# Attention scores from 64-row products, the two maps in the two halves of the rows, in place of stacked 128-row operands

## The chip, the cores and the metric

The kernel runs on one core of one Trainium2 chip. The metric is device time in microseconds (us); less is better. Before the change three runs gave a median of 2869.48 us (2864.72 to 2870.2).

## What is computed

One inference step of a decoder trunk of two layers: a gated linear attention layer and a differential attention layer, each followed by an MLP with squared ReLU and by layer norms. 1024 prompt tokens with 16 meta tokens ahead of them, and 8 single tokens of running sequences, go through. The change lies in the differential attention of the prompt. There each of 8 heads has two maps, each with queries and keys of 64 dimensions:

```python
def diff_core(q, k, v, q_pos, k_pos, lam):
    s = jnp.einsum('bqhmd,bkhmd->bhmqk', q, k).astype(F32) * (DIFF_DH ** -0.5)
    mask = k_pos[None, :] <= q_pos[:, None]
    s = jnp.where(mask, s, -jnp.inf)
    p = jax.nn.softmax(s, axis=-1)
    a = p[:, :, 0] - lam * p[:, :, 1]
    return jnp.einsum('bhqk,bkhe->bqhe', a, v.astype(F32))
```

All data are f32.

## The kernel before, in words

Large products are made from rounded operands: a value is split into `hi`, its cast to the type fp32r, and `lo`, the rest (`split`, L182: a cast on ScalarE, a subtraction on VectorE), and a product of two such values is hi·hi + hi·lo + lo·hi (`mm3`, L186 to L189). Transposes and the products of attention weights with values stay in plain f32.

The stages run in this order: linear attention and its projections; output projection and MLP of the first layer, with the paged attention of the running sequences in the background; the input projection of the second layer (L1098 to L1145); the prompt's differential attention (L1238 to L1275); output projection (`w_out`, L883) and MLP of the second layer. A scheduler orders the instructions of each engine when the program is built, by the order of the code as priority and a time model; each engine then runs its own list in that order. Buffers come from pools, and a buffer is reused when its last reader is done.

Attention goes head by head, and within a head over eight tiles of 128 queries, in the order 7, 1, 5, 3, 6, 0, 4, 2 (L1243; 3, 2, 1, 0, 7, 6, 5, 4 in the last head). Tile t sees 16 + 128 (t + 1) keys.

`prep` (L1063) makes a head's operands. The raw keys and queries (`rqk`, `rkm`) lie with tokens on the partitions; TensorE transposes them into a PSUM bank `axt`, and `split` writes hi and lo with the 128 dimensions on the partitions: map 0 in rows 0 to 63, map 1 in rows 64 to 127. Then six moves for the queries and three for the keys (L1082 to L1084, L1093 to L1095, DMAs on POOL's queue from on-chip memory to itself) stack the operands by map: `k2[m]` holds the key's hi in 64 rows and its lo in the other 64, `q2[m]` the query's hi twice and `ql2[m]` its lo twice. Two products of 128 rows then give all four terms of one map (L1191, L1192). `prep` of the next head is issued at the first two tiles of a head (L1244 to L1249); that of head 0 between blocks of the input projection, whose last blocks are reordered for it (L1099, L1100, L1104). The operands of even and odd heads use different halves of `XH` and `XL`.

`tile_` (L1178) does one tile. Keys are cut into 1 to 3 chunks of at most 512 columns, 14 chunks a head. For each map and chunk: the two products into one PSUM bank `mmt`, and a VectorE reduction (L1195) that adds the mask, scales, writes the scores `as` to on-chip memory and keeps the row's extreme. ScalarE takes the exponentials of both maps (L1197), VectorE combines the maps (L1199 to L1201), TensorE transposes the result in groups of up to four blocks into `axt` (L1210), ScalarE copies these out (L1212), and TensorE multiplies them with the values into `smt` (L1215). After four tiles the results are copied out and their squares are summed (L1260 to L1262). POOL scales finished heads (L1227). In the last head the finished first half is transposed and split for the output projection (`o_fm`, L1229) while the second half runs.

PSUM has eight banks, shared out for the whole kernel: three `mmt` (L123), three `axt` (L124), two `smt` (L125).

Of the kernel before, what the change touches and what calls it, by code (L numbers as in the profile page):

```python
# [11 lines left out]
F32 = mybir.dt.float32  # L12
# [21 lines left out]
NEG = -1e30  # L34
# [77 lines left out]
def hybrid_step(ctx, tc, A, dbg=None, upto=9):  # L112
    nc = tc.nc
# [9 lines left out]
    mm = ctx.enter_context(tc.tile_pool(name="mm", bufs=3, space=PSUM))  # L123
    ax = ctx.enter_context(tc.tile_pool(name="ax", bufs=3, space=PSUM))  # L124
    sm = ctx.enter_context(tc.tile_pool(name="sm", bufs=2, space=PSUM))  # L125

    def mmt():
        return mm.tile([P, 512], F32, name="mmt")

    def axt():  # L130
        return ax.tile([P, 512], F32, name="axt")

    def smt():
        return sm.tile([P, 512], F32, name="smt")

    def cload(name, pool=cp):
        a, b = CCOL[name]
# [44 lines left out]
    def split(hi, lo, src, eng=V):  # L182
        S.copy(hi, src)
        return eng.tensor_tensor(lo, src, hi.bitcast(F32), op=ALU.subtract)  # L184
# [878 lines left out]
    def prep(h, raw, km):  # L1063

        kx, qx = raw[:, 0], raw[:, 1]
        xh, xl = (x.t[h % 2].rearrange("p a n -> p (a n)") for x in (XH, XL))
        w = NM + T
        k2 = [xh[:, :w], xh[:, w : 2 * w]]
        q2 = [xh[:, 2 * w : 2 * w + T], xh[:, 2 * w + T :]]
        kl_, ql2 = xl[:, :w], [xl[:, w : w + T], xl[:, w + T : w + 2 * T]]  # L1070
        kh_ = k2[0]
        move = nc.gpsimd.dma_start
        ps = axt()
        TE.transpose(ps[:, :NM], km, ident[:NM, :NM])
        split(kh_[:, :NM], kl_[:, :NM], ps[:, :NM])
        for c in range(2):
            ps = axt()
            for i in range(4):
                TE.transpose(ps[:, i * P : (i + 1) * P], kx[:, 4 * c + i, :], ident)
            cs = slice(NM + 512 * c, NM + 512 * c + 512)  # L1080
            split(kh_[:, cs], kl_[:, cs], ps)
        move(k2[1][64:], kh_[64:])  # L1082
        move(kh_[64:], kl_[:64])
        move(k2[1][:64], kl_[64:])  # L1084
        yield k2, q2, ql2
        for c in range(2):
            ps = axt()
            for i in range(4):
                TE.transpose(ps[:, i * P : (i + 1) * P], qx[:, 4 * c + i, :], ident)
            cs = slice(512 * c, 512 * c + 512)  # L1090
            split(q2[0][:, cs], ql2[0][:, cs], ps)
        for a, b in (q2, ql2):
            move(b[64:], a[64:])  # L1093
            move(b[:64], a[64:])
            move(a[64:], a[:64])  # L1095
        yield

    units, outs = {}, []  # L1098
    blocks = [(u, t) for u in range(10) for t in range(4)]  # L1099
    blocks += [(10, 0), (10, 1), (10, 2), (11, 0), (11, 1), (10, 3), (11, 2), (11, 3)]  # L1100
    for u, t2_ in blocks:
        if t2_ == 0:
            units[u] = [x.rearrange("p (k n) -> p k n", n=256) for x in kunit(wd, u * 256)]
        if (u, t2_) == (10, 3):  # L1104
            nxt = prep(0, *raws[0])
            with tc.issue_after(outs[-2 * NB]):
                head = next(nxt)
                next(nxt)
        hv, lv = units[u]
        ps = mmt()  # L1110
        for i in range(2):
# [66 lines left out]
    def tile_(h, t, out, vm, vx, k2, q2, ql2):  # L1178
        W = NM + P * (t + 1)
        nch = -(-W // 512)  # L1180
        step = -(-W // nch // 16) * 16
# [3 lines left out]
        mns, neg = st[:, 0, :], st[:, 1, :]  # L1185
        l = ls[:, t, h, :]
        ts_ = slice(t * P, (t + 1) * P)
        for m in range(2):
            for ci, (x, y) in enumerate(cuts):
                ps = mmt()[:, : y - x]  # L1190
                TE.matmul(ps, q2[m][:, ts_], k2[m][:, x:y], start=True, stop=False)  # L1191
                TE.matmul(ps, ql2[m][:, ts_], k2[m][:, x:y], start=False, stop=True)  # L1192
                w = y - x
                mk = cm[:, CW - w :] if y == W else cm[:, 0:1].broadcast_to([P, w])
                V.tensor_tensor_reduce(sc_[:, m, x:y], ps, mk, -0.125, -NEG if ci == 0 else mns[:, m : m + 1], ALU.add, ALU.min, mns[:, m : m + 1])  # L1195
# [39 lines left out]
        V.scalar_tensor_tensor(XL[:, h, cs], ps, gs, XH[:, h, cs].bitcast(F32), ALU.mult, ALU.subtract)  # L1235


    vnxt = load_v(0)  # L1238
    for h in range(8):
        if h:  # L1240
# [32 lines left out]
        o_fm(j, 1)  # L1273
    e.close()
    er.close()  # L1275

# [312 lines left out]
```

## Time and profile before

| | us |
|---|---|
| median of three runs | 2869.48 |
| the profiled execution, its own time | 2879.39 |
| its span, first to last instruction | 2877.6 |
| attention stage, first to last score reduction | 1793 to 2049 |
| busy in the span: TensorE, VectorE, ScalarE, POOL | 2752.2, 1964.2, 1084.7, 1161.8 |

Rows of the profile are read like this. In a group of lines: line, engine, operation, output<-inputs, shapes, count, then busy time and the mean of one in ns, then the idle time of the engine ahead of these instructions and what ended it. In a timeline: start and duration in us, engine, line, operation, tiles, shape, count; in square brackets the idle time before it and its releaser. In the table of stages: the stretch and its length, the busy time and number of instructions of TensorE, its weight loads, VectorE, ScalarE and POOL, then the granted TensorE clock, the DMA engines' busy share and GB/s. In the waits: who waited for whom, us in total, times, longest. PE is TensorE, PEld its weight loads, DVE VectorE, ACT ScalarE. The recorded duration of a matmul includes its way through the array; the pace of a stream is read from start to start.

### The profile page before, as it was taken

To read this page: it belongs to the slowest core of one execution; us is meant where nothing else is said; L and a number is where in the kernel's file an instruction comes from. 1 tells how busy PE (TensorE), PEld (TensorE's weight loads), DVE (VectorE), ACT (ScalarE), POOL (GpSimd) and SP (SyncE) were. 2 spreads that over 40 slices of the span, in tenths; PEclk is the share of its full clock that TensorE was granted. 3 is DMA by queue.
4 is the path that set the end of the run, shared out by engine and by line. 5 is a ranking of instruction groups with operands and counts; after the bars stand their busy time and mean duration, and the time that the engine had idled before them with its cause. 6 is when DMAs were issued, how large, how long until landed. Compare 5 with 4: busy or idle time off the path is not lost.

```text
span 2877.6 us, 51963 instructions
## 1 busy us (share of the span) xinstructions
PE 2752.2 (96%) x19625; PEld 2272.4 (79%) x19625; DVE 1964.2 (68%) x3048; ACT 1084.7 (38%) x2117; POOL 1161.8 (40%) x820
## 2 busy tenths in 40 slices
PE   8889999999999999999999999888999999999997
PEld 5666677997777777777798978878988889797985
DVE  2565544568887787777668721879638887878688
ACT  3233344242221221221341112767515546355553
POOL 1231212234344343433233321123236767777764
PEclk9899999999999999999999999999999999999998
DMA  7557751635798898888568995455334555554574
GB/s 242 181 177 269 253 169 46 238 96 158 283 344 304 311 354 305 329 321 298 213 217 317 360 343 140 107 114 132 119 103 88 110 129 116 132 122 111 130 189 88
DMA packets 277591, 579.66 MB, mean 201 GB/s; under 512 B 24710, under 2 KB 139980, under 8 KB 273244
## 3 DMA queue, kind: packets, MB, share of 16 engines
q1 hardware_dynamic: 252284, 520.66, 52.9%
q0 software_dynamic: 25056, 55.69, 11.1%
q8 instruction: 154, 2.52, 0.4%
q14 instruction: 97, 0.79, 0.1%
HBM read 531.16 MB, written 29.26 MB: 195 GB/s over the span
## 4 chain that ended last, share of the span: by engine, by line
PE 73%; DVE 9%; DMA 8%; issue 5%; POOL 2%; ACT 2%; SPq 0%; DVEq 0%; POOLq 0%; ACTq 0%
PE mmt L187 17%; PE mmt L188 17%; PE mmt L189 17%; PE smt L831 4%; PE axt L187 3%; PE axt L188 3%; PE axt L189 3%; DMA XL<-XL 2%; PE smt L1215 1%; DVE as L1195 1%; DVE pg L790 1%; DMA swt<-in_mlp_w 1%; PE smt L507 1%; DVE as L1201 1%; DMA rw<-in_mlp_w 1%
## 5 line engine op out<-in xcount | busy, mean ns | idle before, releaser
L175 POOL TENSOR_TENSOR wlo<-raw,whi 128x512 fp32r<-128x512 f32 x256 | 366.6, 1445 | 755.9 <-ACT whi L174 678.9
L188 PE MATMUL mmt<-wlo,XH 128*128 128x256 f32 (+1 forms) x1760 | 526.3, 300 | 4.4 <-POOL wlo L175 4.4
L187 PE MATMUL mmt<-whi,XH 128*128 128x256 f32 (+1 forms) x1760 | 525.0, 301 | 2.0 <-ACT Y L311 2.0
L187 PE MATMUL mmt<-XH,whi 128*128 128x512 f32 (+1 forms) x1216 | 436.8, 360 | 5.6 <-DVE HL L184 2.8
L189 PE MATMUL mmt<-whi,XL 128*128 128x256 f32 x1536 | 436.0, 285 | 0.0
L189 PE MATMUL mmt<-XH,wlo 128*128 128x512 f32 (+1 forms) x1216 | 432.9, 356 | 0.0
L174 ACT CAST whi<-raw 128x512 fp32r<-128x512 f32 x256 | 152.8, 619 | 596.4 <-PE mmt L189 185.4
L188 PEld LDWEIGHTS mmt<-wlo,XH 128*128 128x128 f32 x1760 | 333.7, 190 | 32.9 <-issue 17.7
L791 DVE TENSOR_REDUCE sc<-pg 128x16 f32<-128x1024 f32 x256 | 308.3, 1211 | 71.3 <-POOL pg L790 68.8
L187 PEld LDWEIGHTS mmt<-whi,XH 128*128 128x128 f32 x1760 | 332.1, 190 | 26.9 <-issue 12.2
L790 DVE TENSOR_TENSOR pg<-pg,qb 128x1024 f32<-128x1024 f32 x192 | 262.3, 1373 | 70.6 <-DMA pg<-in_cache_k 65.8
L188 PE MATMUL mmt<-XL,whi 128*128 128x512 f32 x768 | 306.2, 399 | 0.0
L189 PEld LDWEIGHTS mmt<-whi,XL 128*128 128x128 f32 x1536 | 291.2, 190 | 8.8 <-issue 8.0
L187 PEld LDWEIGHTS mmt<-XH,whi 128*128 128x128 f32 x1216 | 230.7, 190 | 52.8 <-issue 12.9
L790 POOL TENSOR_TENSOR pg<-pg,qb 128x1024 f32<-128x1024 f32 x64 | 164.3, 2569 | 258.7 <-DMA pg<-in_cache_k 179.9
L189 PEld LDWEIGHTS mmt<-XH,wlo 128*128 128x128 f32 x1216 | 230.7, 190 | 34.5 <-issue 2.1
L187 PE MATMUL mmt<-whi,HH 128*128 128x512 f32 x512 | 205.3, 402 | 4.5 <-DVE Y L1015 4.4
L189 PE MATMUL mmt<-whi,HL 128*128 128x512 f32 x512 | 204.5, 399 | 0.0
L188 PE MATMUL mmt<-wlo,HH 128*128 128x512 f32 x512 | 204.1, 399 | 0.0
L1436 POOL TENSOR_TENSOR wlo<-RW,whi 128x512 fp32r<-128x512 f32 x96 | 174.4, 1840 | 54.5 <-ACT whi L1435 54.5
L1436 POOL TENSOR_TENSOR wlo<-rw,whi 128x512 fp32r<-128x512 f32 x92 | 156.5, 1744 | 83.3 <-ACT whi L1435 68.1
L188 PEld LDWEIGHTS mmt<-XL,whi 128*128 128x128 f32 x768 | 145.0, 189 | 38.3 <-issue 7.1
(434 smaller groups left out, 5827.4 us busy)
## 6 DMA issues: line engine op xcount, KB each, us to landing
pg<-in_cache_k SPq DMA_DIRECT2D x256, 512.0 KB, 6.1
pg<-in_cache_v SPq DMA_DIRECT2D x256, 512.0 KB, 6.3
raw<-in_mlp_w SPq DMA_DIRECT2D x164, 256.0 KB, 4.6
swt<-in_mlp_w SPq DMA_DIRECT2D x32, 1024.0 KB, 5.2
rw<-in_mlp_w SPq DMA_DIRECT2D x116, 256.0 KB, 3.7
RW<-in_mlp_w POOLq DMA_DIRECT2D x96, 256.0 KB, 5.6
raw<-in_gla_w_in SPq DMA_DIRECT2D x48, 256.0 KB, 3.4
swt<-in_gla_w_in SPq DMA_DIRECT2D x12, 1024.0 KB, 5.1
```

Of the source, the lines that this page charges most:

```text
L174: S.copy(hi[:, c], raw)
L175: G.tensor_tensor(lo[:, c], raw, hi[:, c].bitcast(F32), op=ALU.subtract)
L187: TE.matmul(ps, ah, bh, start=first, stop=False)
L188: TE.matmul(ps, ah, bl, start=False, stop=False)
L189: return TE.matmul(ps, al, bh, start=False, stop=last)
L507: TE.matmul(ps[o : o + TS, :], lhs[:, k + i, :], t[:, i, c * 512 : (c + 1) * 512], start=k == 0, stop=k == nk - 2)
L790: eng.tensor_tensor(pg, pg, qb, op=ALU.mult)
L791: return V.tensor_reduce(sc[:, n, :], pg.rearrange("p (h d) -> p h d", d=64), op=ALU.add, axis=AX.X).ins
L831: m = TE.matmul(acc[i * TS : i * TS + 16, :256], w[r, n, :], pg[r, i * 256 : (i + 1) * 256], start=n == 0, stop=n == NPG).ins
L1195: V.tensor_tensor_reduce(sc_[:, m, x:y], ps, mk, -0.125, -NEG if ci == 0 else mns[:, m : m + 1], ALU.add, ALU.min, mns[:, m : m + 1])
L1201: V.scalar_tensor_tensor(sc_[:, 0, :W], sc_[:, 1, :W], neg[:, 0:1], sc_[:, 0, :W], ALU.mult, ALU.add)
L1436: G.tensor_tensor(lo[:, k, :], t, hi[:, k, :].bitcast(F32), op=ALU.subtract)
```

## The change

The stacked operands and the nine moves of each head go. `prep` only transposes and splits, into `ks` (hi and lo of the keys) and `qs` (hi and lo of the queries), one of four pieces at each of a head's tiles 2 to 5; that of head 0 stands whole before the last two blocks of the input projection, whose blocks run in plain order. In `tile_` each chunk has both maps at once: a pair of PSUM banks, and for each of the three terms hi·hi, hi·lo, lo·hi one product of 64 rows for map 0 (rows 0 to 63) and one for map 1 (rows 64 to 127), by turns. The fourth term, lo·lo, is no longer there. The two reductions follow the six products. For the attention stage the PSUM pools are closed and opened anew, as two pairs `prt` (four banks), two `axt` and two `smt`, and after it again as three, three and two.

```diff
+    def open_banks(**counts):
+
+        if banks:
+            banks["stack"].close()
+            banks.clear()
+        banks["stack"] = ctx.enter_context(ExitStack())
+        for name, n in counts.items():
+            banks[name] = banks["stack"].enter_context(tc.tile_pool(name=name, bufs=n, space=PSUM))
+
+    open_banks(mm=3, ax=3, sm=2)
+
+    def pairt():
+        return banks["pr"].tile([P, 2, 512], F32, name="prt")
...
-        k2 = [xh[:, :w], xh[:, w : 2 * w]]
-        q2 = [xh[:, 2 * w : 2 * w + T], xh[:, 2 * w + T :]]
-        kl_, ql2 = xl[:, :w], [xl[:, w : w + T], xl[:, w + T : w + 2 * T]]
...
-        move(k2[1][64:], kh_[64:])
-        move(kh_[64:], kl_[:64])
-        move(k2[1][:64], kl_[64:])
...
-        for a, b in (q2, ql2):
-            move(b[64:], a[64:])
-            move(b[:64], a[64:])
-            move(a[64:], a[:64])
...
+        ks, qs = [xh[:, :w], xl[:, :w]], [xh[:, w : w + T], xl[:, w : w + T]]
         ps = axt()
         TE.transpose(ps[:, :NM], km, ident[:NM, :NM])
+        split(ks[0][:, :NM], ks[1][:, :NM], ps[:, :NM])
+        for x, (hi, lo), at in ((kx, ks, NM), (qx, qs, 0)):
+            for c in range(2):
+                ps = axt()
+                for i in range(4):
+                    TE.transpose(ps[:, i * P : (i + 1) * P], x[:, 4 * c + i, :], ident)
+                cs = slice(at + 512 * c, at + 512 * c + 512)
+                split(hi[:, cs], lo[:, cs], ps)
+                yield ks, qs
...
-    blocks = [(u, t) for u in range(10) for t in range(4)]
-    blocks += [(10, 0), (10, 1), (10, 2), (11, 0), (11, 1), (10, 3), (11, 2), (11, 3)]
-    for u, t2_ in blocks:
+    for u, t2_ in ((u, t) for u in range(12) for t in range(4)):
...
-        if (u, t2_) == (10, 3):
-            nxt = prep(0, *raws[0])
+        if (u, t2_) == (11, 2):
             with tc.issue_after(outs[-2 * NB]):
-                head = next(nxt)
-                next(nxt)
+                head = list(prep(0, *raws[0]))[-1]
...
-        for m in range(2):
-            for ci, (x, y) in enumerate(cuts):
-                ps = mmt()[:, : y - x]
-                TE.matmul(ps, q2[m][:, ts_], k2[m][:, x:y], start=True, stop=False)
-                TE.matmul(ps, ql2[m][:, ts_], k2[m][:, x:y], start=False, stop=True)
...
+        for ci, (x, y) in enumerate(cuts):
+            w = y - x
+            mk = cm[:, CW - w :] if y == W else cm[:, 0:1].broadcast_to([P, w])
+            pair = pairt()
+            pss = [pair[:, m, :w] for m in range(2)]
+            for i, j in ((0, 0), (0, 1), (1, 0)):
+                for m in range(2):
+                    r = slice(64 * m, 64 * m + 64)
+                    TE.matmul(pss[m], qs[i][r, ts_], ks[j][r, x:y], start=i + j == 0, stop=i == 1)
+            for m in range(2):
+                V.tensor_tensor_reduce(sc_[:, m, x:y], pss[m], mk, -0.125, -NEG if ci == 0 else mns[:, m : m + 1], ALU.add, ALU.min, mns[:, m : m + 1])
...
+    open_banks(pr=2, ax=2, sm=2)
     vnxt = load_v(0)
...
                 if n == 0:
                     nxt = prep(h + 1, *raws[h + 1])
+                elif n < 5:
                     hnxt = next(nxt)
-                elif n == 1:
-                    next(nxt)
-                elif n == 3:
+                if n == 3:
                     vnxt = load_v(h + 1)
...
+    open_banks(mm=3, ax=3, sm=2)
```

More of the change, by code (lines that the diff above doesn't have):

```diff
@@ L122, in hybrid_step @@
     wrp = ctx.enter_context(tc.tile_pool(name="wrp", bufs=2))
-    mm = ctx.enter_context(tc.tile_pool(name="mm", bufs=3, space=PSUM))
-    ax = ctx.enter_context(tc.tile_pool(name="ax", bufs=3, space=PSUM))
-    sm = ctx.enter_context(tc.tile_pool(name="sm", bufs=2, space=PSUM))
+    banks = {}
+    def open_banks(**counts):
[8 more added lines that the diff above has]
+        return banks["pr"].tile([P, 2, 512], F32, name="prt")
     def mmt():
-        return mm.tile([P, 512], F32, name="mmt")
+        return banks["mm"].tile([P, 512], F32, name="mmt") if "mm" in banks else pairt()[:, 0]
     def axt():
-        return ax.tile([P, 512], F32, name="axt")
+        return banks["ax"].tile([P, 512], F32, name="axt")
     def smt():
-        return sm.tile([P, 512], F32, name="smt")
+        return banks["sm"].tile([P, 512], F32, name="smt")
     def cload(name, pool=cp):
@@ L1067, in prep @@
         w = NM + T
-        k2 = [xh[:, :w], xh[:, w : 2 * w]]
-        q2 = [xh[:, 2 * w : 2 * w + T], xh[:, 2 * w + T :]]
-        kl_, ql2 = xl[:, :w], [xl[:, w : w + T], xl[:, w + T : w + 2 * T]]
-        kh_ = k2[0]
-        move = nc.gpsimd.dma_start
+        ks, qs = [xh[:, :w], xl[:, :w]], [xh[:, w : w + T], xl[:, w : w + T]]
         ps = axt()
         TE.transpose(ps[:, :NM], km, ident[:NM, :NM])
[L1075 to L1081, printed above, removed]
@@ L1082, in prep @@
-        move(k2[1][64:], kh_[64:])
-        move(kh_[64:], kl_[:64])
-        move(k2[1][:64], kl_[64:])
[L1085 to L1091, printed above, removed]
-        for a, b in (q2, ql2):
-            move(b[64:], a[64:])
-            move(b[:64], a[64:])
-            move(a[64:], a[:64])
@@ L1096, in prep @@
-        yield
+        split(ks[0][:, :NM], ks[1][:, :NM], ps[:, :NM])
[7 more added lines that the diff above has]
+                yield ks, qs
     units, outs = {}, []
-    blocks = [(u, t) for u in range(10) for t in range(4)]
@@ L1176, in load_v, with tile_ @@
         return vm, vx
-    def tile_(h, t, out, vm, vx, k2, q2, ql2):
+    def tile_(h, t, out, vm, vx, ks, qs):
         W = NM + P * (t + 1)
```

3 lines of the change are left out of this document (removed).

## The prediction

> **What bounds the kernel now.** I read the page first, then the attention stage alone, because every line of the diff but one helper lies in it: the busy table by stage, the groups of lines within the stage, the waits, and the timelines of VectorE and TensorE around the first tile of each head.
>
> ```profile
> span 2877.6 us, 51963 instructions
> PE 73%; DVE 9%; DMA 8%; issue 5%; POOL 2%; ACT 2%; SPq 0%; DVEq 0%; POOLq 0%; ACTq 0%
> ```
> ```profile
> 1786.00:1820.00 34.00, 22.92 (x140) 19.95 (x141) 23.25 (x81) 17.59 (x42) 4.79 (x10) 0.87 0.59 136
> ...
> 1793.00:2045.00 252.00, 221.25 (x1546) 201.80 (x1544) 211.75 (x687) 179.47 (x427) 61.36 (x73) 0.94 0.49 112
> ```
>
> Over the whole span the chain is TensorE's. In the attention stage (about 1786 to 2067 us, the second row from the first score reduction to the end of the last head's scores) no engine is full: of 252 us TensorE is busy 221.25 and VectorE 211.75, in records whose TensorE ends are modelled. In the first stretch, with head 0's start, the granted clock is 0.87 against 0.94 over the stage: idle time costs some speed too. Both engines are near the limit, so what counts is which of the idle times end on something that the change removes.
>
> ```profile
> DVE as L1195 <- PE mmt L1192: 35.6, 30, 5.8
> ```
> ```profile
> L1195 DVE CUSTOM_DVE_ANT_0 as<-mmt,cmask 128x352 f32<-128x352 f32 x16 | 8.4, 522 | 22.2 <-PE mmt L1192 22.2
> ```
> ```profile
> 1793.29 0.52 DVE L1195 CUSTOM_DVE_ANT_0 as<-mmt,cmask 128x352 f32<-128x352 f32 x1 [5.79 <-PE mmt L1192]
> ...
> 1822.39 0.52 DVE L1195 CUSTOM_DVE_ANT_0 as<-mmt,cmask 128x352 f32<-128x352 f32 x1 [4.85 <-PE mmt L1192]
> ...
> 1853.76 0.53 DVE L1195 CUSTOM_DVE_ANT_0 as<-mmt,cmask 128x352 f32<-128x352 f32 x1 [2.95 <-PE mmt L1192]
> ...
> 1924.73 0.52 DVE L1195 CUSTOM_DVE_ANT_0 as<-mmt,cmask 128x352 f32<-128x352 f32 x1 [3.92 <-PE mmt L1192]
> ```
>
> VectorE waits 35.6 us for score products. 22.2 us of it stand before one form, the 352-column first chunk, which only tile 7 has, the tile with which heads 0 to 6 begin. The four long waits (17.5 us together) are the starts of heads 0, 1, 2 and 4. What TensorE waits for there:
>
> ```profile
> 1788.67 0.56 PE L1191 MATMUL mmt<-XH 128*128 128x352 f32 x2 [2.68 <-DMA XH<-XH]
> 1792.48 0.96 PE L1192 MATMUL mmt<-XH,XL 128*128 128x352 f32 x2 [3.25 <-DMA XL<-XL]
> ...
> 1819.01 0.63 PE L1191 MATMUL mmt<-XH 128*128 128x352 f32 x1 [3.71 <-issue]
> ...
> 1922.19 0.59 PE L1191 MATMUL mmt<-XH 128*128 128x352 f32 x2 [3.58 <-DMA XH<-XH]
> ```
>
> These are the moves that stack the operands (L1082 to L1084, L1093 to L1095): chains of copies from on-chip memory to itself, issued from POOL. Head 0's chain ends at 1792.48, though the projection before it was done some 8 us earlier:
>
> ```profile
> 1784.41 0.28 PE L188 MATMUL mmt<-wlo,XH 128*128 128x256 f32 x1
> 1784.53 0.28 PE L189 MATMUL mmt<-whi,XL 128*128 128x256 f32 x1
> ```
>
> The 1819.01 wait is put down to "issue", but the move line names its waiters:
>
> ```profile
> L1095 POOL DMA_DIRECT2D XL<-XL x8: 509/512/523, 1785.7 to 2014.3; - x8
> ...
>   PE mmt L1191: 6.3, 2
>   PEld mmt L1192: 6.0, 4
>   PE mmt L1192: 5.0, 4
>   PEld mmt L1191: 3.8, 1
> ```
>
> That is 21.1 us of TensorE waiting for the moves, seen from the other side.
>
> **The moves (removed).** Nine copies a head go, 72 in all, with POOL's 0.51 us for each issue (37 us of POOL, whose 61.36 busy us are not on the path). The transposes, casts and subtractions stay: five pieces a head before and after (16 keys, then four of 512 columns). Their last one is now all that a head's start needs, and they are spread over tiles 2 to 5 of the head before, so it is ready about three tiles early. For head 0 the whole of prep stands before two projection blocks, 2 x 48 matmuls at 0.12 us (start to start in the fence above), 11.5 us, which cover these. I take back 20 of the 22.2 us: a little stays, since a head's first reduction still needs its own products. What is late next is VectorE itself, with 211.75 us of work that the change doesn't touch.
>
> **The products.** Per head and map the keys sum to 8 x 16 + 128 x 36 = 4736 columns. Now: two products of 128 rows, two maps, 18944 columns a head. The steady pace:
>
> ```profile
> 1838.75 0.46 PE L1191 MATMUL mmt<-XH 128*128 128x464 f32 x1
> 1839.05 0.37 PE L1192 MATMUL mmt<-XH,XL 128*128 128x464 f32 x1
> 1839.26 0.37 PE L1191 MATMUL mmt<-XH 128*128 128x448 f32 x1
> 1839.47 0.36 PE L1192 MATMUL mmt<-XH,XL 128*128 128x448 f32 x1
> ```
>
> Start to start 0.21 us for 464 columns, 0.457 ns a column, so 8.66 us a head and 69 us in the stage. Afterwards there are three products of 64 rows per map. If the two halves of the rows run side by side, that is three times instead of four: 52 us, 17 less. If they run one after the other it is six: 104 us, 35 more. No 64-row matmul and none of this rounded type with fewer than 128 rows is in the trace. The nearest rows are two 16-row products in different row groups, in plain f32:
>
> ```profile
> L619 PE MATMUL axt<-gT,wg x16: 587/640/692, 93.7 to 388.1; 16*128 16x512 f32 x16
> ```
> ```profile
> 93.68 0.70 PE L619 MATMUL axt<-gT,wg 16*128 16x512 f32 x2
> ```
>
> Two matmuls, each recorded with at least 0.587 us, lie together within 0.70 us: they run side by side. I take the side-by-side value, with some doubt about the type, and keep both ends. It matters less than it looks: in the forecast VectorE sets the pace, and 17 us fewer on TensorE only shorten the other waits for products (35.6 - 22.2 = 13.4 us at most).
>
> The Trainium skill speaks against this step in TensorEngine Tiling (Array Packing), Key Properties: a change of tiling mode drains TensorE. The row that bears on it is the return from the 16-row products:
>
> ```profile
> 388.58 0.50 PE L187 MATMUL mmt<-XH,whi 128*128 128x512 f32 x1
> 388.92 0.40 PE L188 MATMUL mmt<-XL,whi 128*128 128x512 f32 x1
> 389.15 0.40 PE L189 MATMUL mmt<-XH,wlo 128*128 128x512 f32 x1
> ```
>
> The first slot is 0.34 us, the next 0.23: 0.11 us for the change. Today's scores already pay 0.09 when they follow f32 work (0.30 against 0.21 at 1838.75). If leaving the mode costs another 0.11, that is 112 chunks x 0.11 = 12 us more of TensorE, hidden while VectorE is the bound. By the rule taken alone the sum would be the same with 12 us less reserve; the rule and the row agree that there is a price.
>
> **Banks.** Scores go from three single banks to two pairs, transposes from three to two. A pair holds two reductions, about 1.2 us of VectorE's work, and TensorE refills it in 3 x 0.457 x 338 = 0.46 us plus the signals: no wait of its own. The transposes:
>
> ```profile
> L1212 ACT COPY aT<-axt 128x512 f32<-128x512 f32 (+2 forms) x112 | 51.9, 491 | 41.7 <-PE axt L1210 41.4
> ...
> L184 DVE TENSOR_TENSOR XL<-axt,XH 128x512 fp32r<-128x512 f32 (+1 forms) x34 | 20.1, 593 | 3.1 <-ACT XH L183 3.1
> ```
>
> 112 copies and 34 splits take turns in these banks. With one bank fewer, a transposition can wait for one copy more. Bounds: 0 and 112 x 0.49 = 55 us of TensorE waiting; the lower end is nearer, because copies today wait 41.4 us for transposes and hardly the other way:
>
> ```profile
> PE axt L1210 <- ACT aT L1212: 0.3, 1, 0.3
> ```
>
>  I charge 4 us to the end. Below nothing it can't go.
>
> Between the stages the pools are closed and opened again. That this is no barrier is shown by the pool that replaces the stage's buffers:
>
> ```profile
> L1315 SPq DMA_DIRECT2D rw<-in_diff_w_out x16: 327/364/722, 2001.8 to 2121.6; - x16
> ```
> ```profile
> 2043.13 0.41 PE L1191 MATMUL mmt<-XH 128*128 128x320 f32 x1
> ...
> 2045.79 0.35 PE L187 MATMUL mmt<-whi,XH 128*128 128x256 f32 x1
> ```
>
> Its first load goes out at 2001.8, while the stage that stands before it in the code still computes. And today's output projection starts only after the last scores, so its banks come free at the same point. Nothing is charged; if this were a barrier, the projection would lose its place under the last tiles (2045.8 to 2066), up to 20 us.
>
> **The sum.** -20 (head starts) + 4 (transposes) = -16 us, against the profiled execution's 2879.39 us, 9.9 above the median of the runs shown (2869.48). Carried over to that median: **2853.5 us**. The forecast's own range adds the 13.4 us of other waits below (2840) and 10 us more for banks, mode changes and the order of the instructions, which a scheduler sets anew when the program is built, above (2863.5).
>
> **Rivals.** *The halves run one after the other* (slower). The row for it: none; against it the pair at 93.68. TensorE then has 221 + 35 = 256 us, above VectorE, and becomes the bound. Of its 31 idle us in the stage, some 17 go with the moves and 14 stay: 270 us for 252, less the 6 that head 0's start still gives, +12 us: 2881.5. It decides as soon as a pair of 64-row matmuls takes over about 1.6 times one of them (3 x 1.6 = 4.8 against 4, TensorE then at 235 + 14 us of 252, where hardly anything is left of the gain in the running heads). Chance 0.16.
>
> *Each weight load waits for the matmul in its own half.* A load of 128 columns fits beside a matmul within (1.05 - 0.28) / 7 = 0.11 us today:
>
> ```profile
> 1868.16 1.05 PE L1215 MATMUL smt<-whi,aT 128*128 128x128 f32 x8
> ```
>
>  Unhidden it costs 3 x 0.11 a chunk: 3 x (0.155 + 0.11) = 0.80 us against 0.62 now, 20 us more of TensorE; 241 + 14 is 255 for 252, and with the start's 6 about 2866.5. Against it:
>
> ```profile
> 1000.27 0.50 PE L189 MATMUL mmt<-whi,HL 128*128 128x512 f32 x1
> ```
> ```profile
> 1000.38 0.19 PEld L187 LDWEIGHTS mmt<-whi,HH 128*128 128x128 f32 x1
> ```
>
> The next load runs 0.11 us into a matmul on the same rows. The Trainium skill states the rule in TensorE: Matmul & The Clock Gate, The mechanism: loads overlap running matmuls only where the row group differs. This trace disagrees. Chance 0.06.
>
> *The banks take the gain.* If two transposition banks and pairs held to the end cost 20 us instead of 4, little is left: 2869.5. For it: TensorE issues in order, and everything behind a waiting transposition waits too. Against: the 0.3 us that transposes wait for copies today. Chance 0.10.
>
> *A pool barrier* at the end: 2853.5 + 16 = 2869.5. Chance 0.04.
>
> **Chances.** The forecast holds 0.64. A measurement of this kernel can tell about 0.2% (5.7 us) from no change. Faster by more: nearly all of the forecast and the lucky parts of the rivals, 0.68. Within it: the forecast's high end and the middle of the last three rivals, 0.15. Slower: most of the serial rival and the unlucky parts of the others, 0.17. The range reaches to 2838 below and, with half of the serial rival, to 2882 above.
>
> **What would show it.** Right: no move and no long wait at head starts; the first score reduction within about 2 us of the last projection matmul (1793.3 now); 64-row matmuls of two maps starting a few ns apart, three such pairs in about 0.47 us; VectorE over 90% busy from there to the last scores, which end some 16 us earlier. Wrong: score matmuls start one full matmul apart; VectorE waits for products in the middle of heads; transposes wait for copies; the projection starts after the last transposition. One cause of long waits stays in any case:
>
> ```profile
> 1881.48 1.09 PE L1210 MATMUL axt<-c_ident,as 128*128 128x128 f32 x4 [4.56 <-DVE as L1201]
> ```
>
> It ends on a VectorE pass (L1201) that the change doesn't touch.

## The result, and the profile after

The changed kernel takes 2876.7 us (median of 22 runs) where the kernel before takes 2869.46 (22 runs): 1.0023 times the time, 95% interval 1.0014 to 1.0032. It is slower, by some 7 us; 16 us faster was forecast. The profiled executions differ by 5.5 us in span. First line of the page of after, then two rows of its table of stages: the start, and first score reduction to last scores.

```profile
span 2883.1 us, 52158 instructions
```
```profile
1786.00:1820.00 34.00, 24.48 (x166) 19.93 (x167) 24.20 (x84) 17.79 (x45) 0.00 (x0) 0.78 0.09 24
1791.00:2042.00 251.00, 224.55 (x1757) 182.55 (x1757) 210.47 (x688) 177.60 (x425) 29.04 (x12) 0.95 0.16 46
```

POOL's busy time has halved (29.04 for 61.36) and DMA's share fell from 0.49 to 0.16: the moves are gone. Yet the stage is as long as it was, TensorE is no less busy, and VectorE idles 40.5 of 251 us where it idled 40.3 of 252. One idle time was swapped for another. The groups of VectorE lines in the attention stage of after (busy and mean | idle ahead and its releaser):

```profile
L1195 DVE SCALAR_TENSOR_TENSOR as<-as,ast 128x1040 f32<-128x1040 f32 (+7 forms) x62 | 61.8, 996 | 0.8
L1189 DVE CUSTOM_DVE_ANT_0 as<-prt,cmask 128x272 f32<-128x272 f32 (+5 forms) x128 | 58.6, 495 | 17.5 <-DMA out_v_rows_p<-qo 13.0 <-PE prt L1187 4.5
L1189 DVE CUSTOM_DVE_ANT_0 as<-prt,cmask,ast 128x352 f32<-128x352 f32 (+5 forms) x96 | 52.2, 576 | 10.0 <-PE prt L1187 10.0
L196 DVE TENSOR_TENSOR XL<-axt,XH 128x512 fp32r<-128x512 f32 (+1 forms) x35 | 20.4, 582 | 9.3 <-ACT XH L195 9.3
...
L1256 DVE TENSOR_REDUCE oss<-smt 128x4 f32<-128x512 f32 x15 | 10.4, 693 | 4.8 <-ACT smt L1255 4.8
L1193 DVE RECIPROCAL ast<-ls 128x1 f32<-128x1 f32 x62 | 9.8, 158 | 9.6 <-ACT as L1191 9.3
```

Before, 22.2 us stood ahead of the 352-column first chunk alone, at the starts of heads. Now there are short waits all over: for scores, for the casts of the preparation (L195), for exponentials, for squares, each kind 0.6 to 2 us a head. By heads, VectorE idles 5.0 to 5.5 us in each of heads 1 to 6.

The start kept most of its delay. TensorE has the first scores at once, VectorE does not take them:

```profile
1786.06 0.43 PE L1187 MATMUL prt<-XH 64*128 64x352 f32 x2 [0.72 <-ACT qo L1108]
1786.33 0.32 PE L1187 MATMUL prt<-XL,XH 64*128 64x352 f32 x2
1786.49 0.32 PE L1187 MATMUL prt<-XH,XL 64*128 64x352 f32 x2
```
```profile
1791.31 0.53 DVE L1189 CUSTOM_DVE_ANT_0 as<-prt,cmask 128x352 f32<-128x352 f32 x1 [13.04 <-DMA out_v_rows_p<-qo]
```

The row puts the wait down to the landing of the projection's last output, so some buffer that the reduction needs lies where that output was. Which one is not shown: e8_start, below, moves the score buffers and keeps the wait. From the end of the projection's last output copy it is 5.3 us to this reduction (1786.0 to 1791.3), where it was 7.8 before (1785.5 to 1793.3): behind the wait for the moves stood another. The granted clock of the start fell from 0.87 to 0.78.

The first rows also answer the question of the halves: each row is two matmuls (x2), and the next pair follows 0.16 us later, 0.457 ns by 352. They run side by side, a pair in 0.16 us at this pace; only the first pair holds its slot for 0.27.

Where the difference lies, from the timelines (first and last score reduction; last addition of the output projection; end):

| us | before | after | difference |
|---|---|---|---|
| to the first score reduction | 1793.3 | 1791.3 | -2.0 |
| first to last score reduction | 255.8 | 253.1 | -2.7 |
| from there to the end of the output projection | 127.0 | 136.4 | +9.4 |
| rest | 701.5 | 702.3 | +0.8 |

The forecast put some 6 us of its gain into the first line, the rest into the second, and nothing into the third (a pool barrier there was one of its rivals).

### The profile page after: what moved, and what is told of

Same layout as the page of the kernel before. It is cut to its first block, busy times and chain, and to the rows that moved or that the text cites. A ratio compares the mean times of both kernels' runs of the same rounds, so it can differ in the third digit from the quotient of the medians.

```text
span 2883.1 us, 52158 instructions
## 1 busy us (share of the span) xinstructions
PE 2755.9 (96%) x19849; PEld 2253.8 (78%) x19849; DVE 1987.5 (69%) x3048; ACT 1082.8 (38%) x2117; POOL 1112.3 (39%) x748
## 4 chain that ended last, share of the span: by engine, by line
PE 69%; DVE 14%; DMA 7%; issue 5%; ACT 2%; POOL 2%; SPq 1%; DVEq 0%; POOLq 0%; ACTq 0%
PE mmt L199 17%; PE mmt L200 16%; PE mmt L201 16%; PE smt L843 4%; PE axt L199 2%; PE axt L200 2%; PE axt L201 2%; DVE as L1189 2%; DVE as L1195 1%; DVE pg L802 1%; DMA rw<-in_mlp_w 1%; PE smt L1209 1%; DVE XH L196 1%; ACT as L1191 1%; DVE RX L1406 1%
## 5 line engine op out<-in xcount | busy, mean ns | idle before, releaser
L1431 POOL TENSOR_TENSOR wlo<-RW,whi 128x512 fp32r<-128x512 f32 x96 | 167.7, 1794 | 58.6 <-ACT whi L1430 58.5
```

Source lines behind the costliest of these rows:

```text
L1431: G.tensor_tensor(lo[:, k, :], t, hi[:, k, :].bitcast(F32), op=ALU.subtract)
```

## The experiments

Times are medians with the ratio to the kernel before on the same chip, whose medians there lay between 2869.4 and 2873.1 us; so small differences are read from the ratios; "stage" is first to last score reduction of the profiled execution, "tail" from there to the end of the output projection, "held" what the 64 combinations of two maps take beyond the median of their own length (explained below).

| kernel | us | ratio, 95% interval | stage | held | tail |
|---|---|---|---|---|---|
| before | 2869.5 | 1 | 255.8 | 11.7 | 127.0 |
| after | 2876.7 | 1.0023 (1.0014 to 1.0032) | 253.1 | 10.5 | 136.4 |
| e1_no_moves | 2835.1 | 0.9880 (0.9855 to 0.9905) | 217.4 | 2.7 | 127.5 |
| e2_old_banks | 2881.9 | 1.0035 (1.0019 to 1.0050) | 265.2 | 2.9 | 130.7 |
| e3_singles | 2878.3 | 1.0026 (1.0011 to 1.0040) | 256.5 | 8.0 | 136.4 |
| e4_prep_early | 2874.3 | 1.0006 (0.9992 to 1.0021) | 250.7 | 8.3 | 136.1 |
| e5_form_alone | 2870.4 | 0.9998 (0.9982 to 1.0014) | 254.0 | 0.7 | 130.0 |
| e6_full_rows | 2873.4 | 1.0005 (0.9989 to 1.0021) | 248.0 | 10.6 | 136.9 |
| e8_start | 2869.6 | 0.9995 (0.9980 to 1.0010) | 249.9 | 10.5 | 135.8 |
| e9_doubled | 2870.9 | 0.9994 (0.9979 to 1.0010) | 252.4 | 4.9 | 126.2 |
| e10_pair | 2860.3 | 0.9969 (0.9954 to 0.9984) | 236.6 | 8.6 | 137.3 |
| e11_spread | 2831.5 | 0.9866 (0.9846 to 0.9886) | 218.0 | 0.0 | 126.1 |
| e12_norm_split | 2862.9 | 0.9988 (0.9974 to 1.0001) | 241.4 | 0.0 | 135.2 |
| e13_sum | 2852.4 | 0.9951 (0.9930 to 0.9971) | 243.1 | 0.3 | 128.7 |
| e14_two_banks | 2848.5 | 0.9923 (0.9904 to 0.9942) | 224.3 | 7.7 | 138.8 |
| e15_order | 2834.0 | 0.9878 (0.9857 to 0.9898) | 218.9 | 5.9 | 130.5 |
| e16_three_banks | 2842.8 | 0.9900 (0.9883 to 0.9918) | 238.6 | 0.7 | 126.6 |
| e17_before_split | 2870.0 | 1.0001 (0.9985 to 1.0017) | 253.8 | 8.1 | 127.5 |
| e18_full_early | 2861.2 | 0.9972 (0.9958 to 0.9985) | 236.4 | 8.6 | 136.7 |
| e19_three_early | 2840.0 | 0.9903 (0.9885 to 0.9920) | 231.5 | 1.4 | 127.9 |

**First round: the moves, and the banks undone.** e1_no_moves is the kernel before with

```diff
-        k2 = [xh[:, :w], xh[:, w : 2 * w]]
-        q2 = [xh[:, 2 * w : 2 * w + T], xh[:, 2 * w + T :]]
+        k2 = [xh[:, :w]] * 2
+        q2 = [xh[:, 2 * w : 2 * w + T]] * 2
...
-        move(k2[1][64:], kh_[64:])
...
-            move(a[64:], a[:64])
```

so both maps are computed from the same unstacked operands. It leaves out each map's own scores; so do e6_full_rows, e10_pair, e11_spread, e14_two_banks, e15_order and e18_full_early.

> The kernel before with the nine moves of each head left out and nothing else: both maps then use the same pair of operands, so the scores are those of a sum of both maps and the output is not the reference's; the instructions of all engines but the moves stay. Theory A (the moves' waits were worth what their rows said, and the changed kernel gives it back in its banks): 12 to 20 us below before. Rival B (the waits for moves stood where another wait stands anyway): between 5 below and 2 above.

It saved 34 us, beyond every expectation. Stage row and two groups:

```profile
1790.40:2007.80 217.40, 208.21 (x1575) 194.83 (x1576) 202.65 (x698) 178.64 (x431) 28.76 (x13) 0.99 0.20 58
```
```profile
L1188 DVE CUSTOM_DVE_ANT_0 as<-mmt,cmask 128x272 f32<-128x272 f32 (+5 forms) x128 | 61.6, 494 | 7.3 <-PE mmt L1185 4.4 <-DMA out_v_rows_p<-qo 2.6
```

VectorE is busy 93%, TensorE 96%, the clock is 0.99. Of 38 us less in the stage 25 are VectorE's idle time (40.0 to 14.8) and 9 its held combinations. So the moves were worth more than the waits at the head starts, and the rest of the change must cost some 40 us.

e2_old_banks and e3_singles are the changed kernel with single banks, three for scores and three for transpositions throughout, or four and two (the second part of this edit is e3_singles'):

```diff
-            pair = pairt()
-            pss = [pair[:, m, :w] for m in range(2)]
+            pss = [mmt()[:, :w] for m in range(2)]
...
-    open_banks(pr=2, ax=2, sm=2)
+    open_banks(mm=4, ax=2, sm=2)
```

> The changed kernel with the old banks for the whole kernel: three single score banks, three for transposes, two for results, no pools opened anew; each map's products go to a bank of their own. Theory A (two transposition banks and pairs take the gain): 10 to 18 us below before. Rival B (the place of prep, the halves or a wait that was hidden take it): not more than 3 us below before, about as the changed kernel.

> The changed kernel with four single score banks in place of two pairs, transposes still in two banks. If the release of both banks of a pair at once costs the time: 6 or more us faster than the changed kernel, so at or below before. If the transposition banks do, or neither: as the changed kernel, 5 to 9 us above before.

Both stayed slow, and I took the banks to be cleared. That was too quick: with single banks the second map often has none free and products run alone (355 of 663 in the trace of e2_old_banks, none of 672 in after), so undoing the banks uncovers another cost. In e2_old_banks TensorE is busy 258.75 of 265.2 us.

e4_prep_early prepares in the first two tiles (`if n < 2: next(nxt); hnxt = next(nxt)`).

> The changed kernel with prep of the next head at the first two tiles of a head, where it was before, two pieces at each. If the spread over four tiles puts VectorE's subtractions where it waits for them: 4 or more us faster than the changed kernel. If the two transposition banks are the limit, four pieces close together press harder on them: the same or 2 to 6 us slower.

2874.3 against 2876.7: the intervals overlap.

**Second round: the form of the products.** e5_form_alone is e1_no_moves with the three products of 64 rows, maps by turns, in single banks. e6_full_rows is the changed kernel with products of 128 rows, both maps from the same operands:

```diff
-            for i, j in ((0, 0), (0, 1), (1, 0)):
-                for m in range(2):
-                    r = slice(64 * m, 64 * m + 64)
-                    TE.matmul(pss[m], qs[i][r, ts_], ks[j][r, x:y], start=i + j == 0, stop=i == 1)
+            for m in range(2):
+                for i in range(2):
+                    TE.matmul(pss[m], qs[i][:, ts_], ks[0][:, x:y], start=i == 0, stop=i == 1)
```

> The kernel before with its moves left out (as in e1_no_moves), its old banks, old preparation in two tiles and old block order, but with the three products of 64 rows, the maps by turns, in place of two of 128 rows on operands of one map; both maps correct. It differs from e1_no_moves (2835 us) only in the form of the score products. Theory A (every visit of TensorE to the 64-row form costs some 0.18 us at its two edges, 82 to 112 visits, 15 to 20 us, and VectorE is starved by it): 2860 to 2882. Theory B (the form is cheap; what eats the gain is where the preparation, the blocks and the banks were put): 2833 to 2848.

> The changed kernel with everything as it is (pair banks, preparation over five tiles, plain block order, no moves), but each map's score as two products of 128 rows on the same pair of operands, so both maps get the same scores, which are not the reference's. It differs from the changed kernel (2877) only in the form of the score products. Theory A (the 64-row form): 2832 to 2850, the other edits being worth about 5 us together. Theory B (placement and banks): 2865 to 2880.

Both came out slow, so both theories failed as the only cause: the form alone loses the 34 us, and everything but the form loses them too. Row of e5_form_alone, and some of its score products:

```profile
1786.70:2040.70 254.00, 250.21 (x1778) 205.84 (x1779) 207.55 (x701) 181.21 (x432) 30.73 (x13) 0.96 0.18 50
```
```profile
1859.87 0.45 PE L1188 MATMUL mmt<-XH 64*128 64x384 f32 x1
1860.16 0.33 PE L1188 MATMUL mmt<-XL,XH 64*128 64x384 f32 x1
1860.33 0.34 PE L1188 MATMUL mmt<-XH,XL 64*128 64x384 f32 x1
```

TensorE is full, 250.21 of 254, 42 us more than in e1_no_moves. Part of it is halves that run alone (x1, above), for want of a bank; the pair banks of the changed kernel cure that. The other part is the visit to this form (a visit is a stretch of score products between others). In after, one between output products:

```profile
1901.42 0.83 PE L1209 MATMUL smt<-whi,aT 128*128 128x128 f32 x6
1902.18 0.47 PE L1187 MATMUL prt<-XH 64*128 64x448 f32 x2
1902.49 0.36 PE L1187 MATMUL prt<-XL,XH 64*128 64x448 f32 x2
1902.69 0.37 PE L1187 MATMUL prt<-XH,XL 64*128 64x448 f32 x2
1902.98 0.49 PE L1209 MATMUL smt<-whi,aT 128*128 128x128 f32 x2
```

Six output products at 0.11 us end at 1902.08; the first score starts 0.10 later. Its slot is 0.31 and the last 0.29, where 448 columns stream in 0.20. The first output product behind holds its slot for 0.21 in place of 0.11 (0.49 for two, of which the last is recorded with 0.28). That is 0.1 each on entering, on the first pair, on leaving and on the first product behind (0.06 where that is a transposition), nearly 0.4 us a visit. In e1_no_moves the same edges cancel:

```profile
1850.98 0.60 PE L1079 MATMUL axt<-c_ident,rqk 128*128 128x128 f32 x4
1851.33 0.38 PE L1184 MATMUL mmt<-XH 128*128 128x272 f32 x1
1851.55 0.29 PE L1185 MATMUL mmt<-XH,XL 128*128 128x272 f32 x1
1851.67 0.28 PE L1184 MATMUL mmt<-XH 128*128 128x256 f32 x1
1851.79 0.28 PE L1185 MATMUL mmt<-XH,XL 128*128 128x256 f32 x1
1851.91 1.04 PE L1203 MATMUL axt<-c_ident,as 128*128 128x128 f32 x8
```

The score starts 0.08 before the transpositions' pace would allow (1850.98 + 4 x 0.109), loses 0.09 in its first slot, leaves at its own pace, and so does the transposition behind. In after TensorE visits the scores 79 times between 1795 and 2030 us: 79 x 0.4 = some 30 us, more than the 17 that side by side saves. That the Trainium skill (TensorEngine Tiling (Array Packing), Key Properties) has a mode change drain TensorE agrees with these rows; it gives no price.

e8_start opens the pool of score buffers ahead of its neighbours:

> The changed kernel with the pool of the score buffers opened ahead of its neighbours, so that the first score buffer need not lie on the projection's last output buffer, whose landing the first reduction waited 5.2 us for. If that wait is a cost of its own: 4 to 5 us less than the changed kernel, 2871 to 2874. Rival: another buffer of the new pool then waits for the same landing (the mask or the small tiles), or the projection's tail sets the start anyway: 2875 to 2879.

2869.6 us, 7 less than after, but not for the reason given: its first reduction still waits for the same landing (1780.02, 5.1 us after its scores). Most of the gain lies in the projection, as waits in after (first row) and the groups of TensorE in after and in e8_start show:

```profile
POOL vm L1158 <- SPq L769: 9.4, 1, 9.4
```
```profile
L200 PE MATMUL mmt<-wlo,XH 128*128 128x256 f32 x64 | 18.6, 294 | 3.2 <-POOL wlo L187 3.2
```
```profile
L200 PE MATMUL mmt<-wlo,XH 128*128 128x256 f32 x67 | 19.0, 288 | 0.0
```

In after a clearing of `vm`, which waits for a buffer, stands ahead of the projection's weights on POOL, and TensorE waits for those; in e8_start it does not. Four projection blocks take 36.6 us there, 41.3 in after. The kernel before has this wait too (9.5 us on POOL; the four blocks take 42.4). This edit was not tried on it, so whether the kernel before would gain as much is open; that holds also for the lead of e13_sum, e16_three_banks and e19_three_early, which contain the edit.

e9_doubled keeps products of 128 rows and gets the stack without moves: each map's columns are loaded twice side by side, one transposition fills both halves, casts and subtractions run once a map.

> The kernel before with stacked operands of 128 rows but without moves: each map's 64 columns are loaded twice side by side, one transposition then gives both halves of the rows, and the casts and subtractions run once for each map (4 more casts and 4 more subtractions of 512 columns a head; loads of queries and keys doubled, one buffer instead of two). Theory A (128-row products are the cheap form, the moves cost 34 us, VectorE is the bound without them): 2835 plus 8 heads by 4 subtractions by 0.58 us, some 19 us, and a little more TensorE: 2852 to 2862, faster than both. Theory B (without moves any form ends where the changed kernel does, since the gain of e1_no_moves came from its sharing of operands): 2868 to 2885.

It gained nothing: VectorE is busy 229.7 of 252.4 us and TensorE 231.0, 25 us more VectorE work than in e1_no_moves beside the held time, not 19, and little slack is left. Its first reduction also comes 6 us later than before (1799.3).

**Third round: banks, spread, and a held VectorE.** The mean of L1195 in after is 996 ns, in e1_no_moves 871 for the same forms. In after, POOL and then VectorE:

```profile
1872.71 3.61 POOL L1221 TENSOR_TENSOR Y<-Y,orr 128x2048 f32<-128x2048 f32 x1
```
```profile
1873.11 3.78 DVE L1195 SCALAR_TENSOR_TENSOR as<-as,ast 128x528 f32<-128x528 f32 x1
```

The combination usually takes 0.76 us. It started while GpSimd normalized two heads and ended 0.56 us behind that multiplication; so it went after heads 1, 3 and 5. Reductions from PSUM beside the same multiplication are not held (e1_no_moves, four within it, at their usual length). This is also what ended in the 4.56 us wait for L1201 that the prediction quoted of before. The Trainium skill says the same (SBUF — State Buffer, Who interferes with whom): a VectorE instruction with two inputs in SBUF shuts out, and is shut out by, a GpSimd instruction that reads SBUF. How often it happens is chance of the schedule: 0 to 11.7 us in the column "held". e12_norm_split cuts the multiplication:

```diff
-        eng.tensor_tensor(Yd[:, ts, hs], Yd[:, ts, hs], bc(r, [P, n, m, P], 3), op=ALU.mult)
+        for i in range(n) if eng is G else ():
+            eng.tensor_tensor(Yd[:, i, hs], Yd[:, i, hs], bc(r[:, i], [P, m, P], 2), op=ALU.mult)
```

> The changed kernel with the one multiplication of 2048 columns with which GpSimd normalizes two heads (3.6 us) cut in eight of 256 columns. In the changed kernel's trace a VectorE combination of two maps that starts while that multiplication runs takes 3.77 us in place of 0.76 us and ends 0.56 us behind it, three times, and once 2.77 in place of 1.30. Theory (VectorE is held for as long as one GpSimd instruction): the combinations come back to within 0.5 us of their usual time, 8 to 10 us less VectorE work, 2866 to 2870. Rival (VectorE waits for TensorE instead, since neither is full): 2873 to 2878.

```profile
1864.80 5.95 POOL L1222 TENSOR_TENSOR Y<-Y,orr 128x256 f32<-128x256 f32 x8
```
```profile
1865.20 0.77 DVE L1195 SCALAR_TENSOR_TENSOR as<-as,ast 128x528 f32<-128x528 f32 x1
...
1867.20 1.35 DVE L1195 SCALAR_TENSOR_TENSOR as<-as,ast 128x912 f32<-128x912 f32 x1
```

Held time 10.5 to 0.0, stage 253.1 to 241.4. The other direction shows too: the pieces beside these two combinations took 1.08 and 1.48 us in place of 0.61. The ratios, 0.9988 against 1.0023, put it 10 us below after.

e10_pair is e1_no_moves with the pair banks and the order they bring; e11_spread is e1_no_moves with the preparation spread over tiles 2 to 5.

> e1_no_moves (2835 us: the kernel before without its moves, products of 128 rows, both maps on one pair of operands) with two edits of the change added: the pair banks (two pairs of score banks and two transposition banks in place of three and three, taken back to three behind the heads) and the order that pairs bring, both maps of a stretch of keys ahead of the next stretch. Theory C (banks and order make a ping-pong of TensorE, ScalarE and VectorE, 5 us of idle VectorE a head): 2858 to 2874, with the tail of the stage some 7 us longer as in e6_full_rows. Theory D (they are harmless; the preparation spread over five tiles and the block order cost it): 2833 to 2848.

> e1_no_moves (2835 us) with the preparation of the next head spread over the tiles n = 1 to 4 as in the changed kernel, old banks, old order in a tile, old block order. Theory C (banks and order): 2833 to 2842. Theory D (the spread): 2855 to 2874.

The spread alone costs nothing, the pairs and banks 25 us. e13_sum joins e8_start, e12_norm_split and three transposition banks for the last head:

> The changed kernel with the early pool of score buffers of e8_start, the cut multiplication of e12_norm_split, and three transposition banks for the last head (the banks are opened anew ahead of it, its scores in single banks). If the three costs are separate: 7 for the start, 8 to 10 for the cut, 7 for the tail less up to 3 for the last head's single banks, 2851 to 2860, below both kernels. If a new wait takes their place: 2862 to 2872.

2852.4, as the sum had it.

**Fourth round: which banks, which order.** e14_two_banks is e1_no_moves with `open_banks(mm=4, ax=2, sm=2)` in the stage, e15_order with stretches of keys outside and maps inside.

> e1_no_moves (2835 us) with four score banks, two transposition banks and two output banks in the stage in place of three, three and two, taken back to three, three and two behind it; order and form as before. e10_pair (2860) had two pairs, two transposition banks and the order of pairs at once, and cost 25 us over e1_no_moves, some 7 of them behind the heads. Theory C1 (two transposition banks make the waits of 3.5 us a head): 2850 to 2862. Theory C2 (the order and release in pairs makes them): 2838 to 2846, only the tail longer.

> e1_no_moves (2835 us) with only the order inside a tile changed: stretch by stretch of keys, both maps in each, in place of map by map; banks 3, 3, 2 and single, products of 128 rows. Theory C1 (transposition banks): 2831 to 2840, no cost. Theory C2 (order, since the first map's exponential can start only when nearly the whole tile's scores are reduced): 2845 to 2856.

The order is free. Two transposition banks cost 13 us by the medians; in the profile the tail grows by 11 and the stage by 7, of which 5 are held time. In the tail ScalarE's casts of the outputs wait for transpositions. In after, then in before:

```profile
L1228 ACT ACTIVATE XH<-axt,gs 128x512 fp32r<-128x512 f32 x16 | 11.0, 686 | 11.4 <-PE axt L1227 11.4
```
```profile
L1234 ACT ACTIVATE XH<-axt,gs 128x512 fp32r<-128x512 f32 x16 | 10.9, 689 | 5.2 <-PE axt L1233 5.2
```

e16_three_banks is e13_sum with `open_banks(pr=2, ax=3, sm=1)` for heads 0 to 6:

> e13_sum (2852 us) with three transposition banks and one output bank in heads 0 to 6 in place of two and two. Theory C1 (transposition banks make 3 of the 5 us that VectorE idles in each head): 7 heads by 2 to 3 us less, 2831 to 2840, if the single output bank costs nothing. Theory C2 (order and form): 2848 to 2862, the single output bank adding a wait for its copy and square twice a head.

```profile
L196 DVE TENSOR_TENSOR XL<-axt,XH 128x512 fp32r<-128x512 f32 (+1 forms) x35 | 20.2, 579 | 1.1 <-ACT XH L195 1.1
```

VectorE's waits for casts, 9.3 us in after, are 1.1 here. It leaves nothing out and beats both kernels, by 1.0% and 1.2%, though by less than C1 had it. e17_before_split applies e12's cut to the kernel before:

> The kernel before with GpSimd's multiplication of 2048 columns cut in eight, all else as it is, its moves too. In the trace of before three combinations take 3.9, 5.1 and 5.4 us in place of 0.77, 0.77 and 1.16. Theory (VectorE is the bound between the waits for the moves, so its stalls come off): 7 to 12 us less, 2858 to 2863, so that e13_sum's lead over it is under 12 us. Rival (the moves, which the same queue issues, set the head starts, and the stalls lie in their shadow): 2866 to 2872.

No gain. But the rival isn't shown by it, since the cut did not do its work there: POOL, then VectorE.

```profile
1944.77 4.52 POOL L1228 TENSOR_TENSOR Y<-Y,orr 128x256 f32<-128x256 f32 x7
```
```profile
1944.65 3.60 DVE L1201 SCALAR_TENSOR_TENSOR as<-as,ast 128x528 f32<-128x528 f32 x1
```

Six pieces in a row had started before the combination ended; 8.1 us were held in all. In e12_norm_split two combinations got in after at most one piece. What decides this stays open.

**Last round: the spread beside the pairs.** e18_full_early is e6_full_rows, and e19_three_early e16_three_banks, with the edit of e4_prep_early.

> e6_full_rows (2873 us: the changed kernel with products of 128 rows on one pair of operands) with the preparation back in the first two tiles of the head before. e6_full_rows and e10_pair (2860) share form, pair banks and order and differ in the spread of the preparation and the order of the projection's blocks. If the spread costs what lies between them where pairs and two transposition banks leave little slack: 2858 to 2864. If not, and something else in the operands' layout or the block order does: 2868 to 2876.

> e16_three_banks (2843 us, the fastest kernel so far that computes the reference) with the preparation back in the first two tiles. If the spread costs something beside pair banks even with three transposition banks: 2834 to 2840. If the third bank already gives the slack: 2841 to 2847.

Wait for casts (L196) in e6_full_rows, then in e18_full_early:

```profile
L196 DVE TENSOR_TENSOR XL<-axt,XH 128x512 fp32r<-128x512 f32 (+1 forms) x35 | 20.3, 580 | 11.3 <-ACT XH L195 11.3
```
```profile
L196 DVE TENSOR_TENSOR XL<-axt,XH 128x512 fp32r<-128x512 f32 (+1 forms) x32 | 18.6, 586 | 0.2
```

With two pairs, two transposition banks and products of 128 rows the spread costs 12 us; with three, 2840.0 against 2842.8 is not told apart by the ratios. e19_three_early is the fastest version that leaves nothing out, 0.9903 of the time before.

## Why the prediction was wrong

Stage without the held time, step by step from e1_no_moves to after: 214.7; two transposition banks 216.6; pairs 228.0; spread 237.4; 64 rows 242.6; and the tail goes from 127.5 to 138.8 with the banks and stays near it. Before: 244.1 and 127.0. So leaving out the moves took 29 us from the stage, and the rest of the change put 28 back there and 9 into the tail. The sizes of the steps depend on their order: with the preparation early, products of 64 in place of 128 rows (e18_full_early to e4_prep_early) cost 15 us of stage and 13 by the medians, and the spread (e4_prep_early to after) then next to nothing.

The granted clock moves along: 0.94 over the stage before, 0.95 in after, 0.99 in e1_no_moves, which withholds 15, 13 and 2 us of TensorE time ((1 - clock) x stage). So up to 11 of the 36 us of stage between e1_no_moves and after can have come by way of the clock; no run separates them.

- *"I take back 20 of the 22.2 us"*: the waits at the head starts did go, and more would have: the moves cost 34 us of time, since VectorE idled for TensorE within heads too. But head 0's start gave back 2.5 us only (7.8 to 5.3), because the landing of the last projection output stood behind the moves. I looked for what covers the preparation and not for what else the first reduction needs.
- *"What is late next is VectorE itself"*: this is the step that failed. VectorE has 210 us of work and TensorE 224 of 251 in records; with both near the limit each chain through ScalarE and the banks shows. VectorE did not become the bound: in after neither is full and 40 us are lost in short waits; in e1_no_moves VectorE idles 14.8.
- *"Banks ... I charge 4 us to the end"*, from 0.3 us of transpositions waiting for copies: mis-sized. A wait that is not there with three banks does not bound the wait with two. Two transposition banks alone cost 13 us, pairs with them 12 more, the spread beside both 12 to 13 (medians of e14_two_banks, e10_pair, e6_full_rows, e18_full_early). The 25 us of banks and pairs lie about halfway to the upper bound, 55 us. The rival that the banks take the gain, 0.10, named one right place.
- *The products*: side by side was right, down to the 4 ns or so between starts. The price of the mode was taken as 0.11 us and *"hidden while VectorE is the bound"*; it is nearly 0.4 us a visit, some 30 us, and eats the 17. The 0.09 that the prediction charged to today's scores is made up by their earlier start. From e6_full_rows to after, which changes only the form, the form costs 3 us by the medians (the intervals overlap) and 5 in the stage; from e18_full_early to e4_prep_early, the same step with the preparation early, 13 (the intervals lie apart) and 15.
- The serial halves and the weight loads didn't happen: pairs follow each other at 0.457 ns a column. *A pool barrier*: the tail did grow by 9.4 us, but the projection kept its place beside the last tiles. In after it starts 0.2 us behind the last score reduction, and 26 us ahead of the last output products:

```profile
2044.59 0.56 PE L199 MATMUL mmt<-whi,XH 128*128 128x256 f32 x1 [0.91 <-DVE ast L1193]
...
2070.53 0.61 PE L1209 MATMUL smt<-whi,aT 128*128 128x128 f32 x4
```

  Before, it started 3.3 us ahead of the last reduction (2045.8, 2049.1) and had 28 more products done by then, at 0.12 us some 3 of the 9.4. Whether the opening behind the stage or the two transposition banks of the last head set it back is not shown: every run with two such banks there opens its banks anew behind the stage, e14_two_banks too. e16_three_banks opens its banks ahead of the last head, with three for transpositions, and has no growth.
- My first theory was the banks, and after e2_old_banks I dropped it for the form alone; e5_form_alone and e6_full_rows showed that each suffices. Not shown is whether pairs cost their 12 us by releasing two maps at once or by leaving transpositions too few banks: the third bank (e16_three_banks against e13_sum) brings 5 us of stage back.

## What to carry to other kernels

An edit that frees one engine's wait is worth what the next chain allows: count every wait that ends within a few us of the one removed, and treat banks lost in the same change as lost latency cover, even where today's trace shows no wait for them. Where several parts each suffice to lose the gain, undoing one part from the changed kernel shows nothing; adding the parts one by one to the best version does. Halves of TensorE's rows pay only for long visits: here a chunk of three pairs lasts half a microsecond and the edges of a visit nearly 0.4.

## What the hardware showed that was not expected

- One GpSimd multiplication of 2048 columns held a VectorE instruction with two SBUF inputs for 3.0 us (3.78 for 0.76), three times in a stage; cut into 0.6 us pieces it held none in e12_norm_split, and in e17_before_split one that took 3.60 us while six pieces started.
- Matmuls of 64 rows of this rounded type run in both halves at once, some 4 ns apart, at the full pace of 0.457 ns a column, and cost 0.1 us each at the entry, at the first pair, at the exit and at the first output product behind.
- The granted clock was 0.78 (after) and 0.87 (before) over the 34 us at the start, where TensorE was busy 24.5 and 22.9, and 0.99 over the stage of e1_no_moves, where it was busy 96%.
